# A transformer layer on one core: where the first stage's weight scans and gate sums stand, and which engine makes the bounds of w2 and w_out

## The chip, the core and the metric

The kernel runs on one core of a Trainium2 chip. A core has five engines that run their own queues in order and meet only at semaphores: TensorE (PE: matmul and transpose, into PSUM), VectorE (DVE), ScalarE (ACT), GpSimd (POOL) and SyncE (SP, which here issues most DMAs). An instruction at the head of a queue that waits holds up everything behind it on that engine. The metric is the device time of one execution in microseconds (us); lower is better. All times here are from runs on the chip, and the trace is one profiled execution.

## The reference

One layer (`DEPTH` = 1) with 2048 latent rows and 256 context rows of width 1024. Two mixers read the same projection `h @ w_in`: a retention (linear attention with decay, both directions) and a grouped-query attention; their outputs are joined and go through `w_out`, then a squared-ReLU MLP follows.

```python
mod = (c_act @ w_mod + b_mod)[:, None, :]
sh1, sc1, g1, sh2, sc2, g2 = jnp.split(mod, 6, axis=-1)
h = _modulate(_rmsnorm(x, norm1_g), sh1, sc1)
rq, rk, rv, rg, aq, ak, av = jnp.split(h @ w_in, SPLIT_IDX, axis=-1)
...
x = x + g1 * (jnp.concatenate([ret, att], axis=-1) @ w_out)
h2 = _modulate(_rmsnorm(x, norm2_g), sh2, sc2)
x = x + g2 * _sqrelu_mlp(h2, w_ff1, w_ff2)
```

The context rows need only the columns rk, rv, ak and av.

## The kernel before

The kernel has three stages. The first, some 672 us long, makes `h @ w_in` and everything that later stages need beforehand. The second is the attention with the retention beside it, the third the MLP. The later stages are written out by hand in a fixed order (`manual_schedule`); the first is not. There the program is written as loops, and a list scheduler at build time decides each engine's order: it takes instructions forward as soon as what they need, their buffers among it, is free in its own plan. An operation that depends on nothing but a load and a buffer can so be placed far ahead of the place where it is written.

**Groups and chunks.** The 18 tiles of 128 rows go in three groups: G0 is two context tiles and four latent ones, G1 and G2 are six latent tiles each (`GROUPS`). For each group the columns of w_in are passed in six chunks (`PLAN`): AKV (256 columns: ak and av), AQ, RK, RV, RQ and RG (512 each). G0 begins with RK; G2 ends with RG, RQ. One chunk of one tile, here called a product, is 24 matmuls (`products`, L824 to L826: eight slices of the inner dimension, in three parts of a split into a high and a low half) into one of five PSUM banks `pso`. Then `post` takes it out: an ACT copy `xs` (L524 for RK and RQ, L552 for RV, L556 for RG, L565 for AQ, L586 for AKV), a rotation on DVE and POOL (`rope`, L489 to L496), head norms for AQ and AKV, transposes on PE a tile later (`turn`) and stores by SP.

**What DVE does in this stage.** Beside the rotations: the low halves of the weights (`split_w`, L67, `wlo`), the low halves and the modulation of the next group's `h` (`part_h`, L436 and L67, `lo`), and three kinds of work that no product of this stage needs:

- `weight_maxima`: 72 pieces of weights, 32 of w1, 32 of w2 and 8 of w_out. Each is a DMA of 512 KB into a buffer `wm` (two of them) and a DVE maximum of absolute values into one column of `wmx` (L662). `ff_scales` reads the columns at the start of G2's last chunk and makes powers of two of them, by which the operands of the later stages are scaled.
- `mod_steps`: the later rows of the modulation (gates, second shift and scale). Each is a chain of 16 multiply-adds over a DMA'd piece of w_mod (L354, L356, `macc`), closed by a matmul that sums it over the partitions (L368).
- in G2 alone the attention's values, the decay tables and the first maxima of the attention: `first_maximum` puts 18 pairs of a PE product (L165, L169) and a DVE maximum `nm` (L178) beside G2's last chunks. All 18 share one PSUM bank, so each product waits for the maximum before it.

The loop over chunks and tiles calls one step of `mods` for each tile from G0's second chunk on, apart from G0's last two, and one step of `maxima` for each tile from G1 on (two for the first tile of a chunk):

```python
if mods and (g, c) >= (0, 1) and (g, c) not in ((0, 4), (0, 5)):
    mods.pop(0)()
if (g, c) >= (1, 0):
    for step in maxima[: 1 + (m == 0)]:
        step()
```

The scheduler does not keep the maxima there: a piece depends on its load and on `wm` alone, so in the built program the first stands among G0's first products and the last in G1's RV.

Of the kernel before, what the change touches and what calls it, by code (L numbers as in the profile page):

```python
# [14 lines left out]
BF16 = mybir.dt.bfloat16  # L15
I32 = mybir.dt.int32
AF = mybir.ActivationFunctionType
ALU = mybir.AluOpType
AX = mybir.AxisListType
# [3 lines left out]
P = 128  # L23
D = 1024
# [18 lines left out]
C_RQ, C_RK, C_RV, C_RG, C_AQ, C_AKV = 0, 512, 1024, 1536, 2048, 2560  # L43
# [11 lines left out]
def layer_kernel(ctx: ExitStack, tc: tile.TileContext, a: dict, out: bass.AP):  # L55
    nc = tc.nc
# [56 lines left out]
    wmx = const.tile([P, 88], F32, name="wmx")  # L113
# [27 lines left out]
    class Group:  # L141
# [18 lines left out]
        def piece(self, i, pool=None, tag="mp"):  # L160
            m = self.m[i] = (pool or psS).tile([P, 512], F32, name="mp", tag=tag)
            h, r = i // 9 * 2, i % 9
            if r < 8:
                k = ks[:, self.g, r % 4 * 512 : (r % 4 + 1) * 512]
                mm(m, self.qr[:, 0, h + r // 4], k, start=True, stop=True)  # L165
            else:
                for e in range(2):
                    k = ks[:, self.g, 2048:]
                    mm(m[:, 256 * e : 256 * e + 256], self.qr[:, 0, h + e], k, start=True, stop=True)  # L169
# [90 lines left out]
    with ExitStack() as st:  # L260
# [131 lines left out]
        def mod_steps():  # L392
            steps = later_rows(4, lambda b: store_gate(0, b)) + later_rows(6, shift2)
            return steps + later_rows(8, scale2) + later_rows(10, lambda b: store_gate(1, b))
# [255 lines left out]
        def weight_maxima():  # L650


            def piece(i):
                w = sg.tile([P, D], F32, name="wm", tag="wm", bufs=2)
                if i < 32:
                    src = a["w_ff1"][0, i // 4 * P : (i // 4 + 1) * P, i % 4 * D : (i % 4 + 1) * D]
                elif i < 64:
                    src = a["w_ff2"][0, (i - 32) * P : (i - 31) * P, :]
                else:
                    src = a["w_out"][0, (i - 64) * P : (i - 63) * P, :]  # L660
                nc.sync.dma_start(w, src)
                nc.vector.tensor_reduce(wmx[:, i : i + 1], w, axis=AX.X, op=ALU.max, apply_absolute_value=True)  # L662

            return [lambda i=i: piece(i) for i in range(72)]

        def ff_scales():

# [213 lines left out]
        hs, w, begun = start()  # L881
# [3 lines left out]
        balance(g2)  # L885
        todo = [(g, c) for g in range(len(GROUPS)) for c in range(len(PLAN[g]))]
        spare = []
        mods = mod_steps()
        maxima = weight_maxima()
        beside = None  # L890
        for n, (g, c) in enumerate(todo):
            if (g, c) == (2, 1):
                spare += value_parts()
            if (g, c) == (2, 2):
                spare += decay_tables()
            if (g, c) == (2, 5):
                spare += ff_scales()
            col, width = PLAN[g][c]
            last = c == len(PLAN[g]) - 1
            more = g + 1 < len(GROUPS)  # L900
            w_next = None
            if n + 1 < len(todo):

                w_next = load_w(*PLAN[todo[n + 1][0]][todo[n + 1][1]], range(0, KT if n else 4, 2))
            if more and (c == len(PLAN[g]) - 2):
                loads, xs = load_x(GROUPS[g + 1])
                for load in loads:
                    load()
            nxt = []
            for m, (kind, i) in enumerate(GROUPS[g]):  # L910
                if not (kind == "c" and col in (C_RQ, C_RG, C_AQ)):
                    ps, k = (begun.pop(m), 6) if n == 0 and m in begun else (None, 4)
                    if ps is None:
                        ps = psO.tile([P, 512], F32, name="pso", tag="pso")
                        products(ps, hs[m], w, width, range(4))
                    if beside:
                        next(beside, None)
                    products(ps, hs[m], w, width, range(k, KT))
                    todo_ = later[:]
                    later.clear()  # L920
                    post(col, kind, i, ps)
                    for fn in todo_:
                        fn()
                    if spare:
                        spare.pop(0)()
                    if mods and (g, c) >= (0, 1) and (g, c) not in ((0, 4), (0, 5)):
                        mods.pop(0)()
                    if (g, c) >= (1, 0):
                        for step in maxima[: 1 + (m == 0)]:
                            step()  # L930
                        del maxima[: 1 + (m == 0)]
                    if (g, c, m) == (2, 2, 0):
                        beside = first_maximum()
                if n == 0 and m == len(GROUPS[g]) - 1:
                    w_next += load_w(*PLAN[0][1], range(4, KT, 2))
                if last and more:
                    nxt += make_h(GROUPS[g + 1][m : m + 1], xs[m : m + 1])
            w = w_next
            if last and more:
                hs = nxt  # L940
# [867 lines left out]
```

## Time and profile before

| | |
|---|---|
| median of three runs | 2945.95 us (2940.34 to 2947.11) |
| profiled execution | 2946.76 us |
| its span, first to last instruction | 2945.0 us |
| PE busy | 2776.2 us (94%) |
| DVE busy | 2181.6 us (74%) |
| ACT busy | 1388.0 us (47%) |
| POOL busy | 1550.2 us (53%) |
| DVE maxima of weights (L662) | 72 of 1.211 us, 36 us to 343 us from the start |
| mean granted TensorE clock | 0.987 |

How to read it: an engine's busy time is the sum of its instructions. A PE that is busy all the time need not be at its peak, since a matmul's end is modelled and matmuls overlap; the distance between the starts of two of them is the better measure. Rows of a timeline give start, duration, engine, line, operation, result and operand, count, and in brackets how long the engine sat idle just before and what ended that. Rows of windows give, for each stretch, its length, the busy time (and number) of PE, PE's weight loads, DVE, ACT and POOL, the granted clock, the share of the 16 DMA engines and the GB/s; for a single line they give that engine alone. Rows of waits give total, times and longest.

### The profile page before, as it was taken

What the parts mean: (1) busy time and instruction counts of PE and PEld (TensorE: products, weight loads), DVE (VectorE), ACT (ScalarE), POOL (GpSimd) and SP (SyncE); (2) the same over time, 40 slices, a digit from 0 to 9 for tenths busy, and PEclk for the clock granted to TensorE, in tenths of its full rate; (3) what the DMA queues carried; (4) which work ended last, traced back from release to release, by engine and by line L of the source; (5) the groups of instructions that cost most, each with busy time, mean ns of one, the idle gap of its engine ahead of it and who ended that gap; (6) DMA issues with size and microseconds to landing.
All of it is one profiled execution on the core that took longest, in us unless ns stands there. A gap on an engine that the chain in (4) does not pass through costs nothing. (4 is left out here: it accounts for less than half of the span.)

```text
span 2945.0 us, 45295 instructions
## 1 busy us (share of the span) xinstructions
PE 2776.2 (94%) x17140; PEld 1648.8 (56%) x17140; DVE 2181.6 (74%) x3330; ACT 1388.0 (47%) x2280; POOL 1550.2 (53%) x1274
## 2 busy tenths in 40 slices
PE   7998898998799999999999899999999899999998
PEld 3777677775566666565666444444444344444443
DVE  5889847647987777777876577778777777777776
ACT  2333323325777777787777433333332333333332
POOL 3536326425876667887656656664443444444332
PEclk9999999999999999999999999999999999999999
DMA  9988843426412123332211723331114511111111
GB/s 300 340 283 280 271 154 107 160 67 201 137 46 81 49 63 121 90 104 85 73 63 51 273 92 101 104 102 60 53 51 154 173 60 47 54 51 51 58 44 58
DMA packets 265305, 346.95 MB, mean 118 GB/s; under 512 B 106231, under 2 KB 163831, under 8 KB 263294
## 3 DMA queue, kind: packets, MB, share of 16 engines
q1 hardware_dynamic: 254806, 336.57, 35.2%
q10 hardware_dynamic: 10280, 7.48, 0.9%
q8 instruction: 135, 2.21, 0.3%
q14 instruction: 84, 0.69, 0.1%
HBM read 272.52 MB, written 71.46 MB: 117 GB/s over the span
## 5 line engine op out<-in xcount | busy, mean ns | idle before, releaser
L178 DVE TENSOR_REDUCE nm<-mp 128x1 f32<-128x512 f32 (+1 forms) x576 | 390.9, 685 | 172.6 <-PE mp L165 143.3
L219 POOL TENSOR_TENSOR plo<-p,phi 128x1024 f16<-128x1024 f32 x160 | 353.7, 2212 | 172.9 <-ACT phi L212 139.6
L208 ACT ACTIVATE p<-st 128x512 f32<-128x512 f32 x576 | 338.1, 597 | 188.5 <-PE st L203 118.7
L1582 PE MATMUL pd<-w2hi,uhi 128*128 128x512 f16 x1024 | 388.0, 379 | 12.9 <-DVE acc L1585 12.6
L1583 PE MATMUL pd<-w2lo,uhi 128*128 128x512 f16 x1024 | 388.0, 379 | 0.6 <-DVE w2lo L71 0.6
L1584 PE MATMUL pd<-w2hi,ulo 128*128 128x512 f16 x1024 | 388.1, 379 | 0.0
L1585 DVE SCALAR_TENSOR_TENSOR acc<-pd,sc,acc 128x512 f32<-128x512 f32 x512 | 366.4, 739 | 5.7 <-PE pd L1584 5.6
L1522 PE MATMUL pu<-hf,w1f 128*128 128x512 f16 x896 | 340.1, 380 | 2.5 <-DVE q L1545 2.0
L1523 PE MATMUL pu<-hf,w1f 128*128 128x512 f16 x896 | 340.0, 379 | 0.0
L1524 PE MATMUL pu<-hf,w1f 128*128 128x512 f16 x896 | 339.8, 379 | 0.0
L824 PE MATMUL pso<-whi,hi_l 128*128 128x512 f32 (+1 forms) x768 | 295.8, 388 | 10.2 <-ACT xs L524 4.3
L212 ACT ACTIVATE phi<-p 128x1024 f16<-128x1024 f32 x288 | 303.8, 1055 | 0.0
L826 PE MATMUL pso<-whi,lo_l 128*128 128x512 f32 (+1 forms) x768 | 293.7, 383 | 4.1 <-DVE lo_l L67 4.1
L825 PE MATMUL pso<-wlo,hi_l 128*128 128x512 f32 (+1 forms) x768 | 292.9, 382 | 0.8 <-DVE wlo L67 0.7
L235 PE MATMUL o<-wv,plo 128*128 128x65 f16 x2304 | 235.9, 193 | 23.9 <-POOL plo L219 17.0
L221 DVE TENSOR_TENSOR plo<-p,phi 128x512 f16<-128x512 f32 x256 | 240.9, 942 | 18.6 <-ACT phi L212 15.7
L236 PE MATMUL o<-wv,phi 128*128 128x129 f16 x2304 | 243.8, 221 | 0.0
L235 PEld LDWEIGHTS <-plo 128*128 128x128 f16 x2304 | 206.7, 98 | 59.8 <-POOL plo L219 25.9
L202 PE MATMUL st<-qr,ks 128*128 128x512 f16 x576 | 220.2, 382 | 12.4 <-ACT p L208 10.4
L1534 POOL TENSOR_TENSOR r<-r 128x512 f32<-128x512 f32 x64 | 66.3, 1039 | 295.2 <-ACT r L1533 295.2
L203 PE MATMUL st<-qr,ks 128*128 128x512 f16 x576 | 220.0, 382 | 0.1
L165 PE MATMUL mp<-ks,qr 128*128 128x512 f16 x512 | 196.7, 384 | 23.0 <-DVE nm L178 22.2
(324 smaller groups left out, 5751.4 us busy)
## 6 DMA issues: line engine op xcount, KB each, us to landing
wm<-in_w_ff SPq DMA_DIRECT2D x64, 512.0 KB, 5.3
w1r<-in_w_ff SPq DMA_DIRECT2D x64, 512.0 KB, 4.6
ws<-in_w_ff SPq DMA_DIRECT2D x124, 256.0 KB, 3.5
wst<-in_w_in SPq DMA_DIRECT2D x60, 512.0 KB, 5.5
wst<-in_w_mod SPq DMA_DIRECT2D x32, 512.0 KB, 6.0
hf<-hp SPq DMA_DIRECT2D x56, 256.0 KB, 3.2
hf<-hf SPq DMA_DIRECT2D x14, 1024.0 KB, 7.1
orv<-rv SPq DMA_DIRECT2D x35, 256.0 KB, 4.0
```

Source lines behind the costliest of these rows:

```text
L178: nc.vector.tensor_reduce(dst, src, axis=AX.X, op=ALU.max, negate=True)
L208: nc.scalar.activation(self.p[kt // 2][:, kt % 2], self.s.pop(kt), AF.Exp, scale=HD**-0.5)
L212: nc.scalar.activation(hi, self.p[j], AF.Copy)
L219: nc.gpsimd.tensor_tensor(lo, p, hi, op=ALU.subtract)
L235: mm(o[:, : HD + 1], lo[:, i, c], v[:, : HD + 1], start=False, stop=False)
L1522: mm(pu[i], whi, hi, start=k == 0, stop=False)
L1523: mm(pu[i], whi, lo, start=False, stop=False)
L1524: mm(pu[i], wlo, hi, start=False, stop=k == 3)
L1582: mm(ps, uh, wh, start=f == 0, stop=False)
L1583: mm(ps, uh, wl, start=False, stop=False)
L1584: mm(ps, ul, wh, start=False, stop=f == NF - 1)
L1585: nc.vector.scalar_tensor_tensor(acc[:, c], ps, sc2, acc[:, c], op0=ALU.mult, op1=ALU.add)
```

## The change

Three things, all in the first stage.

- The 40 pieces of w2 and w_out are no longer scanned for a maximum on DVE. ACT takes the absolute value of each piece with its accumulator on (L668), so that the column holds the sum of magnitudes of a row, which bounds the maximum from above. The elementwise result goes into `junk`, a buffer of one that the squares of `load_x` and the head norms use too. The load into `wm` stays.
- The 32 maxima of w1 (L665) and all of `mod_steps` become one list, `extra`, with the mod steps first. Each slot (a tile of a chunk from G0's second chunk to G2's RG) earns credit in proportion to a number given for its chunk (`ROOM`; less where the next group's `h` is made beside it), and steps are taken from the list while the credit lasts. AKV earns nothing.
- The bounds on ACT are called one for each tile from G1 on, except in AKV.

Since `wm` has two buffers and `junk` one, and both are now shared by instructions of two engines in the order of the program, the scheduler can't take the w1 maxima ahead of the bounds that come before them.

```diff
                 nc.sync.dma_start(w, src)
-                nc.vector.tensor_reduce(wmx[:, i : i + 1], w, axis=AX.X, op=ALU.max, apply_absolute_value=True)
-
-            return [lambda i=i: piece(i) for i in range(72)]
+                to = wmx[:, i : i + 1]
+                if i < 32:
+                    nc.vector.tensor_reduce(to, w, axis=AX.X, op=ALU.max, apply_absolute_value=True)
+                else:
+                    junk = tp.tile([P, D], BF16, name="junk", tag="junk", bufs=1)
+                    nc.scalar.activation(junk, w, AF.Abs, accum_out=to)
+
+            steps = [lambda i=i: piece(i) for i in range(72)]
+            return steps[:32], steps[32:]
...
-        mods = mod_steps()
-        maxima = weight_maxima()
+        ROOM = {C_AKV: 0.0, C_AQ: 0.2, C_RK: 1.2, C_RV: 4.2, C_RQ: 3.4, C_RG: 3.2}
+        maxima, bounds = weight_maxima()
+        extra = [(1.56, fn) for fn in mod_steps()] + [(1.2, fn) for fn in maxima]
+
+        def room(g, c):
+            v = ROOM[PLAN[g][c][0]]
+            return v - 2.2 if c == len(PLAN[g]) - 1 and g + 1 < len(GROUPS) else v
...
+        slots = [(g, c) for g, c in todo if (0, 1) <= (g, c) < (2, 5)]
+        share = sum(x for x, _ in extra) / sum(room(*s) * len(tiles_of(*s)) for s in slots)
+        credit = 0.0
...
-                    if mods and (g, c) >= (0, 1) and (g, c) not in ((0, 4), (0, 5)):
-                        mods.pop(0)()
-                    if (g, c) >= (1, 0):
-                        for step in maxima[: 1 + (m == 0)]:
-                            step()
-                        del maxima[: 1 + (m == 0)]
+                    if (g, c) in slots:
+                        credit += share * room(g, c)
+                        while extra and credit > -0.01:
+                            cost, fn = extra.pop(0)
+                            credit -= cost
+                            fn()
+                        if g > 0 and col != C_AKV and bounds:
+                            bounds.pop(0)()
```

In the built program the change shows at three places. The first is DVE's queue where G0's RG meets G1's first chunk. `t` and `lo` belong to the next group's `h`, `wlo` to the next chunk's weights, `wmx<-ys` to RG's own rows. Before:

```order
L436 TENSOR_TENSOR t<-psx,a_237 128x512 x2
L662 TENSOR_REDUCE wmx<-wm 128x1 x2
L67 TENSOR_TENSOR lo_l_2108<-t,hi_l_2107 128x512
L67 TENSOR_TENSOR lo_l_2130<-t,hi_l_2129 128x512
L662 TENSOR_REDUCE wmx<-wm 128x1
L436 TENSOR_TENSOR t<-psx,a_237 128x512
L662 TENSOR_REDUCE wmx<-wm 128x1
L67 TENSOR_TENSOR wlo<-wst,whi 128x2x256
L559 TENSOR_REDUCE wmx<-ys 128x1
```

Now the same place, with the multiply-adds of the modulation between:

```order
L436 TENSOR_TENSOR t<-psx,a_237 128x512
L356 SCALAR_TENSOR_TENSOR macc<-wst,cc,macc 128x512
L67 TENSOR_TENSOR lo_l_2117<-t,hi_l_2116 128x512
L356 SCALAR_TENSOR_TENSOR macc<-wst,cc,macc 128x512
L67 TENSOR_TENSOR lo_l_2139<-t,hi_l_2138 128x512
L436 TENSOR_TENSOR t<-psx,a_237 128x512
L67 TENSOR_TENSOR lo_l_2139<-t,hi_l_2138 128x512
L436 TENSOR_TENSOR t<-psx,a_237 128x512
L559 TENSOR_REDUCE wmx<-ys 128x1
```

The maxima of weights are gone from between the steps of `h`: from G0's RG to the end of G1's AKV before has 16 of them, the program now none, with about as many multiply-adds (8 and 6).

The second place is ACT's queue in G1's RK. `xs` takes a product out of PSUM, `zs` a transposed tile; `qh` is AQ's. Before:

```order
L577 ACTIVATE qh<-psx 128x512
L66 ACTIVATE whi<-wst 128x1024 x2
L546 ACTIVATE zs<-psx 128x512
L515 DMA rtb<-in_ret_cs 128x256
L524 ACTIVATE xs<-pso 128x512
L546 ACTIVATE zs<-psx 128x512
```

Now:

```order
L668 ACTIVATE junk,wmx<-wm 128x1024
L577 ACTIVATE qh<-psx 128x512
L524 ACTIVATE xs<-pso 128x512
L668 ACTIVATE junk,wmx<-wm 128x1024
L546 ACTIVATE zs<-psx 128x512
L515 DMA rtb<-in_ret_cs 128x256
L668 ACTIVATE junk,wmx<-wm 128x1024 x2
```

From G1's AQ to its RV the queue now holds 26 such bounds, one or two ahead of each copy.

The third place is DVE's queue in G2's RV, where the first maxima of the attention (`nm`) run. Before:

```order
L496 TENSOR_TENSOR ys<-t_5644,t_5645 128x512
L178 TENSOR_REDUCE nm<-mp 128x1 x5
L67 TENSOR_TENSOR wlo<-wst,whi 128x1024
L178 TENSOR_REDUCE nm<-mp 128x2
L67 TENSOR_TENSOR wlo<-wst,whi 128x1024 x3
```

Now:

```order
L178 TENSOR_REDUCE nm<-mp 128x1
L496 TENSOR_TENSOR ys<-t_5639,t_5640 128x512
L665 TENSOR_REDUCE wmx<-wm 128x1
L178 TENSOR_REDUCE nm<-mp 128x1
L665 TENSOR_REDUCE wmx<-wm 128x1
L178 TENSOR_REDUCE nm<-mp 128x1
L665 TENSOR_REDUCE wmx<-wm 128x1 x2
L178 TENSOR_REDUCE nm<-mp 128x1
L665 TENSOR_REDUCE wmx<-wm 128x1 x3
```

Of the 32 maxima of w1, 29 now stand after the first product of G2's RK, 24 of them in RV and RG, each waiting for a load of its own; three stand in G1's RQ. Of the 64 multiply-adds, 16 stand in G1's RQ and RG, where before had 4.

More of the change, by code (lines that the diff above doesn't have):

```diff
@@ L887, in layer_kernel, with tiles_of @@
         spare = []
-        mods = mod_steps()
-        maxima = weight_maxima()
+        ROOM = {C_AKV: 0.0, C_AQ: 0.2, C_RK: 1.2, C_RV: 4.2, C_RQ: 3.4, C_RG: 3.2}
[4 more added lines that the diff above has]
+            return v - 2.2 if c == len(PLAN[g]) - 1 and g + 1 < len(GROUPS) else v
+        def tiles_of(g, c):
+            return [t for t in GROUPS[g] if not (t[0] == "c" and PLAN[g][c][0] in (C_RQ, C_RG, C_AQ))]
+        slots = [(g, c) for g, c in todo if (0, 1) <= (g, c) < (2, 5)]
+        share = sum(x for x, _ in extra) / sum(room(*s) * len(tiles_of(*s)) for s in slots)
+        credit = 0.0
         beside = None
@@ L896, in layer_kernel @@
             if (g, c) == (2, 5):
+                assert not extra and not bounds, (len(extra), len(bounds))
                 spare += ff_scales()
```

## The prediction

> **What bounds the kernel now.** I read the page's slices first, to see where PE is not full, then tables by stretches of the first stage, and then the waits and the timeline inside the worst stretch.
>
> ```profile
> PE 2776.2 (94%) x17140; PEld 1648.8 (56%) x17140; DVE 2181.6 (74%) x3330; ACT 1388.0 (47%) x2280; POOL 1550.2 (53%) x1274
> ...
> PE   7998898998799999999999899999999899999998
> ...
> DVE  5889847647987777777876577778777777777776
> ```
>
> A slice is 73.6 us. PE is the bound nearly everywhere; its weak slices are the first nine, and there, in slices 2 to 4, DVE is at eight and nine tenths. To cut the first stage into chunks I use ACT's copies out of `pso`: the first copy of a chunk marks where its first product has ended.
>
> ```profile
> 204.85 0.59 ACT L556 ACTIVATE xs<-pso 128x512 f32<-128x512 f32 x1
> ...
> 277.83 0.60 ACT L565 ACTIVATE xs<-pso 128x512 f32<-128x512 f32 x1 [4.24 <-PE pso L826]
> ...
> 398.50 0.60 ACT L524 ACTIVATE xs<-pso 128x512 f32<-128x512 f32 x1 [5.36 <-DMA rv<-xs]
> ...
> 431.85 0.60 ACT L556 ACTIVATE xs<-pso 128x512 f32<-128x512 f32 x1 [3.29 <-PE pso L826]
> ...
> 490.36 0.60 ACT L565 ACTIVATE xs<-pso 128x512 f32<-128x512 f32 x1 [2.85 <-PE pso L826]
> ...
> 536.67 0.60 ACT L524 ACTIVATE xs<-pso 128x512 f32<-128x512 f32 x1 [0.83 <-PE pso L826]
> 573.50 0.60 ACT L552 ACTIVATE xs<-pso 128x512 f32<-128x512 f32 x1 [3.02 <-PE pso L826]
> ...
> 591.09 0.60 ACT L552 ACTIVATE xs<-pso 128x512 f32<-128x512 f32 x1 [5.12 <-PE pso L826]
> 596.80 0.60 ACT L552 ACTIVATE xs<-pso 128x512 f32<-128x512 f32 x1 [5.12 <-PE pso L826]
> 609.51 0.60 ACT L556 ACTIVATE xs<-pso 128x512 f32<-128x512 f32 x1
> 642.52 0.60 ACT L524 ACTIVATE xs<-pso 128x512 f32<-128x512 f32 x1 [5.11 <-PE pso L826]
> ```
>
> The rows at 591.09 and 596.80 are two products that wait for PE alone: one product of 512 columns takes 5.71 us, one of 256 half of that, 2.86. That is the yardstick. Now the busy times, first of all work (PE, weight loads, DVE, ACT, POOL), then of the weight maxima alone (DVE):
>
> ```profile
> 0.00:85.00 85.00, 66.65 (x328) 38.57 (x329) 47.36 (x100) 26.24 (x50) 23.79 (x43) 0.98 0.93 315
> 85.00:204.85 119.85, 113.87 (x584) 93.48 (x583) 108.08 (x144) 46.07 (x81) 59.21 (x64) 1.00 0.91 306
> 204.85:277.83 72.98, 63.27 (x331) 52.31 (x330) 67.42 (x97) 21.82 (x44) 38.93 (x46) 0.91 0.90 297
> 277.83:398.50 120.67, 110.41 (x480) 86.50 (x479) 86.50 (x111) 39.76 (x61) 44.36 (x44) 0.94 0.75 244
> 398.50:469.40 70.90, 68.84 (x355) 56.93 (x354) 39.98 (x52) 23.81 (x38) 34.53 (x29) 1.00 0.40 121
> 469.40:536.67 67.27, 59.32 (x314) 50.63 (x313) 51.46 (x123) 31.55 (x68) 43.60 (x55) 0.95 0.31 90
> 536.67:672.00 135.33, 133.91 (x613) 106.72 (x612) 63.71 (x126) 34.00 (x49) 35.13 (x36) 1.00 0.38 123
> ```
>
> ```profile
> 0.00:85.00 85.00, 12.10 (x10) 0.98 0.93 315
> 85.00:204.85 119.85, 33.18 (x28) 1.00 0.91 306
> 204.85:277.83 72.98, 22.46 (x19) 0.91 0.90 297
> 277.83:398.50 120.67, 19.35 (x16) 0.94 0.75 244
> ```
>
> From 85 to 278 us DVE is busy 90 to 92% of the time, and a third of that is weight maxima; from 398 us on there are none and DVE has room. One maximum is 1.21 us, one multiply-add of the modulation 0.78:
>
> ```profile
> L662 DVE TENSOR_REDUCE wmx<-wm 128x1 f32<-128x1024 f32 x72 | 87.1, 1211 | 14.8 <-DMA wm<-in_w_ff 11.4 <-DMA wm<-in_w_out 3.3
> ...
> L356 DVE SCALAR_TENSOR_TENSOR macc<-wst,cc,macc 128x512 f32<-128x512 f32 x56 | 43.7, 781 | 7.9 <-DMA wst<-in_w_mod 7.2
> ```
>
> In the worst stretch, G0's RG and G1's AKV (204.85 to 277.83), PE's waits all lead back to DVE's queue:
>
> ```profile
> PE pso L826 <- DVE lo_l L67: 4.1, 3, 2.0
> PE pso L824 <- ACT hi_l L66: 2.6, 2, 2.2
> PE psx L434 <- DVE t L436: 2.0, 2, 1.7
> ```
>
> `lo` and `t` are the next group's `h`, and the ACT operation between them waits for `t` by way of POOL. The waits are 8.7 us, yet the stretch loses more, because TensorE runs at half pace after them:
>
> ```profile
> 238.29 0.58 PE L826 MATMUL pso<-whi,lo_l 128*128 128x256 f32 x1 [2.00 <-DVE lo_l L67]
> 238.67 0.41 PE L824 MATMUL pso<-whi,hi_l 128*128 128x256 f32 x1
> 238.88 0.41 PE L825 MATMUL pso<-wlo,hi_l 128*128 128x256 f32 x1
> ...
> 242.09 0.28 PE L824 MATMUL pso<-whi,hi_l 128*128 128x256 f32 x1
> 242.22 0.28 PE L825 MATMUL pso<-wlo,hi_l 128*128 128x256 f32 x1
> ```
>
> Starts are 0.21 us apart after the wait of 2.00 us, 0.12 to 0.13 us apart three and a half us later; the stretch's granted clock is 0.91.
>
> **The change part by part.** The sum is made against the profiled execution's 2946.76 us, which is 0.8 us over the median of the runs, 2945.95.
>
> *Term 1, G0's RG and G1's AKV.* The same pair of chunks in the next group, RG and AKV from 431.85 to 490.36, has no weight maxima and takes 58.5 us with two products of 512 columns more, so 58.5 - 2 x 5.71 = 47.1 us is what 73.0 us would come down to. DVE's part falls from 67.4 by the 22.5 us of maxima to 45, with about as many multiply-adds as before. 45 of 47 us is tight, so I leave 4 us of waits: 73 - 51 gives -22. Bounds: -26 (no wait left) and -9 (only the waits named go, the clock stays).
>
> One rule of the Trainium skill speaks against the larger value: TensorE: Matmul & The Clock Gate, Part 1, says that the clock falls to half after an idle window of about 3.4 us, and no wait here is longer than 2.2. By it the half pace would have another cause and would stay, and the term would be 0.09 x 73 = 6.6 us smaller, -15. The trace shows the half pace right behind waits of 2 us, so I do not follow it.
>
> *Term 2, G1's AQ, RK and RV* (277.83 to 398.50, 120.7 us). G2's RK and RV, 536.67 to 609.51, take 36.4 us each without maxima; three such are 109.2. DVE loses 16 maxima (19.4 us) and a dozen multiply-adds. ACT gains 26 bounds. The nearest operation in the trace is the square with accumulator over the same 1024 columns, with its read:
>
> ```profile
> L410 ACT ACTIVATE junk<-x_l x16: 1039/1057/1061, 23.4 to 320.3; 128x1024 bf16<-128x1024 f32 x16
> L410 ACT ACTIVATION_READ_ACCUMULATOR junk<-x_l x16: 185/186/203, 24.4 to 321.3; 128x1 f32 x16
> ```
>
> 26 x 1.24 = 32 us raises ACT from 40 to 72 of 110 us, so the time itself is covered by PE. What is behind each bound on ACT is a copy out of `pso` or `psx`; five `pso` banks are 28 us of cover for the first, two `psx` banks little for the second. So -10, with bounds -15 and +16 (below).
>
> *Term 3, the first 205 us.* 85.00 to 204.85 holds some six small and fifteen large products, 6 x 2.86 + 15 x 5.71 = 103 us of 120, some 5 us of it finishing RK. DVE falls from 108 to 75 us, 90% to 62%. Of about 12 us I take 8 (two thirds, as DVE is not the only thing late there). In the first 85 us ten maxima and their 5.2 MB of DMA leave, at 315 GB/s 17 us of DMA time; but PE's clock there is 0.98, and the loads that go ahead were queued behind those that PE needs. I take 0, bounds 0 and -6. Term 3 is -8, from -18 to 0.
>
> *Term 4, G1's RQ and RG.* DVE gains 12 multiply-adds of 0.78 us and three maxima, 13 us on 40 of 71; PE covers it. ACT gains four bounds, 5 us on 24. G2's AKV and AQ lose nothing, since no maxima were there, and gain five bounds on ACT, 6 us on 32 of 67. 0 for both.
>
> *Term 5, G2's RK, RV, RG and RQ.* 29 maxima of 1.21 us put 35 us on DVE's 64 of 135, which PE's pace covers, provided that their loads come in time: RV and RG hold 24, from 573.50 to 642.52, 2.9 us each. Two buffers give one piece per half of (landing + 1.21).
>
> ```profile
> DMA to landing us min/median/max: 3.3/5.3/9.1
> ...
> DMA to landing us min/median/max: 4.1/5.1/5.3
> ```
>
> The first row is `wm` as it was loaded before, between full DMA engines; the second is w_in's pieces of the same size from 529 to 640 us, the nearer one. By 3.3, 4.1, 5.1 and 9.1 us a piece takes 2.3, 2.7, 3.2 and 5.2 us; 24 pieces are late by 0, 0, 7 and 55 us. Lateness counts because the attention's first maxima (`nm`) and the next `wlo` stand behind a waiting piece on DVE, and PE's next L165 waits for `nm`. The median row is of loads issued in threes and fours at once; these go one by one, so I lean to 4.1 and take +4, bounds 0 and +55. SP's queue holds the same loads between the stores of rv and rg, where each can hold them back for a us or two: inside the +4. POOL's queue holds none of it.
>
> The Trainium skill, DMA: Bandwidth & Descriptors, Anatomy of one DMA, fits a DMA on GpSimd's path as 2.0 us and the bytes at 436 GB/s. An estimate by that page is 3.2 us for 512 KB, and by it term 5 would be 0. The shortest row, 3.3 us, agrees; the medians do not.
>
> *Term 6, the later stages.* Their order is written by hand and unchanged; the scales are read from the same columns at the start of RQ. 0.
>
> Sum: -22 - 10 - 8 + 0 + 4 = -36, so 2946.76 - 36 = 2910.8, and by the median's 0.8 less 2910.0.
>
> **The rivals.**
> *ACT takes the wait over.* If the bounds wait for loads as long as 7 us, RK's twelve take 12 x (7 + 1.24) / 2 = 49 us in a chunk of 36, and the transposes' copies wait behind them. Then term 2 turns to 0, and term 3 and 5 halve and double: -22 - 4 + 8 = -18, 2928. For it: ACT and DVE now share two buffers in one order, and `wm` did land as late as 9.1 us. Against it: that was between full DMA engines, and from 277.83 to 398.50 the DMA share was 0.75 with 16 pieces of `wm` in it; there will be 26, but they are called one a tile, not as fast as buffers come free.
> *A larger gain.* All of the room between the stretches and their yardsticks is taken, -26 - 15 - 18 = -59, and loads come in time: 2887. For it speaks DMA's 0.93 at the start; against it that DVE stays tight in term 1.
> *The loads of w1 pace G2 and the kernel is slower.* With 9.1 us of landing RV and RG last 55 us longer: -40 + 55 = +15, 2961. It decides from (69 + 40) / 24 x 2 - 1.21 = 7.9 us of landing on. For it: DVE waits in order and a single PSUM bank ties PE to it. Against it: the DMA share is 0.38 there, where nothing landed later than 5.3 us.
> *Nothing.* The waits go by POOL instead, which stands between `t` and `hi`, and DVE's relief is hidden: 2946. Against it: POOL is busy 38.9 of 73 us.
>
> **How the numbers follow.** The forecast (2900 to 2922) 0.53, ACT's waits 0.18, the larger gain 0.11, nothing 0.05, slower 0.13. Under 0.3%, 9 us, a measurement of this kernel can hardly tell from no change. Faster is 0.53 + 0.18 + 0.11 = 0.82, same 0.05, slower 0.13. The range leaves out the slower case, nothing, and the end of the larger gain: 2891 to 2936.
>
> **What would show it.** Right: from G0's RG to G1's AQ some 50 us instead of 73 and a clock near 1.00 there; DVE at 60 to 65% from 85 us to RG; G1's chunks as long as G2's; PE's end of the first stage near 636 us. Wrong: ACT's bounds waiting for `wm` with PE's transposes behind; DVE's L665 waiting for DMA in G2's RV and RG by more than a few us, and L165 behind L178.

## The result and the profile after

| | before | after |
|---|---|---|
| median of ten runs each | 2946.48 us (2940.34 to 2949.63) | 2952.84 us (2948.55 to 2961.59) |
| span of the profiled execution | 2945.0 us | 2950.2 us |
| ratio after / before | | 1.0031, 95% interval 1.0021 to 1.0041 |

The changed kernel is slower by 0.31%, where 1.2% faster was forecast. The page of the changed kernel, engines and slices:

```profile
PE 2769.6 (94%) x17140; PEld 1643.3 (56%) x17140; DVE 2151.8 (73%) x3290; ACT 1430.9 (49%) x2360; POOL 1555.0 (53%) x1274
...
PE   7999998988789998999999899999999999999998
...
DVE  4668468667987777777877477778777777777776
```

DVE's load did move: its slices 2 to 4 (eight, eight and nine tenths before) are at six, six and eight. PE's eights in the fourth and fifth slice are gone, but the ninth, 590 to 664 us, has become one. The first copies of the chunks out of `pso`, cut as in the prediction (ACT's timeline of the changed kernel):

```profile
202.13 0.60 ACT L556 ACTIVATE xs<-pso 128x512 f32<-128x512 f32 x1 [1.70 <-DMA qt<-zs]
...
256.24 0.58 ACT L565 ACTIVATE xs<-pso 128x512 f32<-128x512 f32 x1
...
375.87 0.58 ACT L524 ACTIVATE xs<-pso 128x512 f32<-128x512 f32 x1
...
447.41 0.39 ACT L586 ACTIVATE xs<-pso 128x256 f32<-128x256 f32 x1 [0.51 <-PE pso L833]
...
523.40 0.59 ACT L524 ACTIVATE xs<-pso 128x512 f32<-128x512 f32 x1
...
646.79 0.60 ACT L524 ACTIVATE xs<-pso 128x512 f32<-128x512 f32 x1 [6.11 <-PE pso L833]
...
676.85 0.60 ACT L524 ACTIVATE xs<-pso 128x512 f32<-128x512 f32 x1 [3.08 <-PE pso L833]
```

The last row is the last copy of the stage; before it stood at 672.1 us. By stretches between these rows (us):

| stretch | before | after | moved | forecast |
|---|---|---|---|---|
| to G0's RG (term 3) | 204.8 | 202.1 | -2.7 | -8 |
| G0's RG, G1's AKV (term 1) | 73.0 | 54.1 | -18.9 | -22 |
| G1's AQ, RK, RV (term 2) | 120.7 | 119.6 | -1.0 | -10 |
| G1's RQ, RG (term 4) | 70.9 | 71.5 | +0.6 | 0 |
| G2's AKV, AQ (term 4) | 67.3 | 76.0 | +8.7 | 0 |
| G2's RK, RV, RG and RQ to the last copy (term 5) | 135.4 | 153.4 | +18.0 | +4 |
| from the last copy to the end of the span (term 6) | 2272.9 | 2273.4 | +0.5 | 0 |

The sum is +5.2 us, the difference of the spans (the medians differ by 6.4). Busy times of the changed kernel in the same stretches (PE, weight loads, DVE, ACT, POOL, then clock, DMA share, GB/s):

```profile
85.00:202.13 117.13, 113.51 (x579) 93.41 (x578) 80.60 (x120) 45.48 (x79) 53.43 (x61) 0.99 0.62 195
202.13:256.24 54.11, 48.74 (x296) 42.64 (x295) 42.65 (x67) 20.84 (x41) 38.85 (x45) 0.97 0.62 192
256.24:375.87 119.63, 111.82 (x502) 86.56 (x501) 68.22 (x88) 67.56 (x116) 47.86 (x45) 1.00 0.79 263
375.87:447.41 71.54, 69.47 (x347) 56.43 (x347) 50.83 (x62) 25.40 (x42) 31.95 (x27) 1.00 0.66 219
447.41:523.40 75.99, 66.82 (x349) 56.18 (x349) 61.65 (x133) 38.73 (x79) 48.69 (x60) 0.96 0.50 132
523.40:646.79 123.39, 107.73 (x450) 84.31 (x449) 72.62 (x85) 31.15 (x47) 23.68 (x20) 0.93 0.74 241
```

The seam between G0 and G1 did what term 1 says: 54.1 us, clock 0.97. The last row is the new worst stretch: PE is busy 107.7 of 123.4 us, DVE only 72.6, and the clock is 0.93. DVE is not full there, it waits. The waits of that stretch, and the landings of `wm` in it:

```profile
DVE wmx L665 <- DMA wm<-in_w_ff: 40.7, 24, 3.6
ACT junk L668 <- DMA wm<-in_w_out: 11.1, 3, 4.5
PE mp L165 <- DVE nm L178: 9.6, 5, 3.7
```

```profile
DMA to landing us min/median/max: 4.5/5.3/7.4
```

24 maxima wait for their loads, 40.7 us in all, and five times PE waits for a maximum of the attention (`nm`) that stands right behind one of them. DVE's timeline in G2's RG shows the order:

```profile
612.09 1.22 DVE L665 TENSOR_REDUCE wmx<-wm 128x1 f32<-128x1024 f32 x1 [2.33 <-DMA wm<-in_w_ff]
615.48 1.22 DVE L665 TENSOR_REDUCE wmx<-wm 128x1 f32<-128x1024 f32 x1 [2.17 <-DMA wm<-in_w_ff]
616.62 0.68 DVE L178 TENSOR_REDUCE nm<-mp 128x1 f32<-128x512 f32 x1
```

And PE's timeline behind that `nm`:

```profile
617.36 0.38 PE L165 MATMUL mp<-ks,qr 128*128 128x512 f16 x1 [2.52 <-DVE nm L178]
...
620.20 0.63 PE L831 MATMUL pso<-whi,hi_l 128*128 128x512 f32 x1
620.62 0.63 PE L832 MATMUL pso<-wlo,hi_l 128*128 128x512 f32 x1
...
621.68 0.40 PE L832 MATMUL pso<-wlo,hi_l 128*128 128x512 f32 x1
621.92 0.40 PE L833 MATMUL pso<-whi,lo_l 128*128 128x512 f32 x1
```

A wait of 2.5 us is followed by some 3.5 us in which matmuls start 0.42 us apart instead of 0.23: the half pace that the prediction showed at the seam before now stands in G2.

### The profile page after: what moved, and what is told of

Read it like the earlier page. It is cut to its first block, busy times and chain, and to the rows that moved or that the text cites. A ratio compares the mean times of both kernels' runs of the same rounds, so it can differ in the third digit from the quotient of the medians.

```text
span 2950.2 us, 45373 instructions
## 1 busy us (share of the span) xinstructions
PE 2769.6 (94%) x17140; PEld 1643.3 (56%) x17140; DVE 2151.8 (73%) x3290; ACT 1430.9 (49%) x2360; POOL 1555.0 (53%) x1274
## 5 line engine op out<-in xcount | busy, mean ns | idle before, releaser
L235 PEld LDWEIGHTS <-plo 128*128 128x128 f16 x2304 | 205.6, 98 | 58.6 <-POOL plo L219 26.0
L202 PE MATMUL st<-qr,ks 128*128 128x512 f16 x576 | 219.0, 380 | 16.5 <-ACT p L208 16.3
L1558 POOL TENSOR_TENSOR r<-r 128x512 f32<-128x512 f32 x64 | 66.4, 1041 | 294.5 <-ACT r L1557 294.5
```

The lines of the kernel that those rows point to most:

```text
L235: mm(o[:, : HD + 1], lo[:, i, c], v[:, : HD + 1], start=False, stop=False)
```

## The experiments

Verdicts of single runs go by the end of the first stage (its last copy), because the rest of the program, which is the same everywhere, took from 2272.6 to 2282.1 us in the profiled executions. Four kernels built nearly alike up to G2's RK reach it at 523.4, 526.2, 527.7 and 528.6 us, so a difference below some 5 us at that place says little. In every run the stretches are cut at the same copies (us):

| kernel | time | to G0's RG | G0 RG, G1 AKV | G1 AQ to RV | G1 RQ, RG | G2 AKV, AQ | G2 RK to RG | last copy |
|---|---|---|---|---|---|---|---|---|
| before | 2946.5 | 204.8 | 73.0 | 120.7 | 70.9 | 67.3 | 105.8 | 672.1 |
| after | 2952.8 | 202.1 | 54.1 | 119.6 | 71.5 | 76.0 | 123.4 | 676.9 |
| w1_eight_columns | 2953.8 | 204.5 | 56.5 | 118.8 | 71.0 | 77.0 | 112.6 | 669.9 |
| w1_eight_loads | 2938.9 | 202.9 | 56.3 | 118.9 | 74.9 | 73.1 | 103.2 | 659.5 |
| halves | 2942.3 | 200.1 | 55.8 | 117.1 | 72.3 | 79.0 | 113.4 | 667.6 |
| w1_noop | 2936.4 | 205.1 | 55.2 | 120.4 | 73.6 | 74.2 | 102.2 | 660.4 |
| no_w1 | 2923.2 | 197.4 | 52.1 | 116.4 | 70.6 | 72.6 | 108.1 | 646.6 |
| no_scans_after | 2924.5 | 199.2 | 51.5 | 107.1 | 76.2 | 71.6 | 106.1 | 641.2 |
| before_no_scans | 2918.9 | 194.3 | 54.0 | 113.2 | 72.9 | 69.6 | 109.2 | 643.0 |
| before_act | 2935.4 | 203.1 | 55.5 | 114.1 | 71.5 | 74.4 | 106.2 | 654.4 |
| before_act_in_place | 2929.9 | 210.0 | 69.9 | 100.3 | 72.2 | 65.6 | 107.2 | 654.8 |
| in_place | 2937.3 | 220.2 | 64.0 | 100.3 | 77.2 | 67.9 | 106.4 | 665.6 |
| gate | 2948.9 | 194.0 | 58.1 | 137.4 | 66.4 | 80.6 | 103.8 | 669.9 |
| w1_in_g1 | 2937.3 | 194.9 | 58.6 | 137.8 | 57.4 | 72.9 | 108.1 | 659.7 |
| before_act_halves | 2936.4 | 206.7 | 66.2 | 108.6 | 71.3 | 68.0 | 106.0 | 656.4 |

The theories, as the expectations name them: LOADS (w1's loads, through two buffers, set the pace of G2), ACT (the sums on ScalarE wait for loads and for the shared scratch `junk`, with the copies behind them), WORK (VectorE's own time for the scans).

### What costs in G2: four edits of the changed kernel

*w1_eight_columns*: loads kept, the scans nearly taken away; 1016 of 1024 columns are left out of w1's bound.

```diff
-nc.vector.tensor_reduce(to, w, axis=AX.X, op=ALU.max, apply_absolute_value=True)
+nc.vector.tensor_reduce(to, w[:, :8], axis=AX.X, op=ALU.max, apply_absolute_value=True)
```

> The changed kernel, with each maximum of w1 taken over the first 8 of its 1024 columns (the other 1016 are left out of the bound); every load of 512 KB stays and DVE waits for it as before. Theory LOADS (G2 is late because DVE stands waiting for w1's pieces, which two buffers deliver one in 3.2 us, with nm and wlo behind it): G2's RG stays near 47 us, and the kernel near 2950, 2944 to 2953. Theory WORK (the 35 us of DVE work of these maxima make G2 late): RG falls to some 35 us and the kernel to 2925 to 2932.

*w1_eight_loads*: the scans kept, three loads of four taken away; 24 pieces of w1 are left out of its bound.

```diff
+kept = []
 def piece(i):
+    if i < 32 and i % 4:
+        nc.vector.tensor_reduce(
+            wmx[:, i : i + 1], kept[0], axis=AX.X, op=ALU.max, apply_absolute_value=True
+        )
+        return
     w = sg.tile([P, D], F32, name="wm", tag="wm", bufs=2)
+    kept[:] = [w]
...
```

> The changed kernel with all its 32 maxima of w1 on VectorE, but a load for every fourth alone: each loaded piece is scanned four times (24 of 32 pieces of w1 are left out). 28 of these maxima now stand in G2's RK and RV, one to RG. LOADS (the pace of w1's loads through two buffers, with the attention's `nm` and `wlo` behind on VectorE): the stage ends like the version without w1's scans, last copy at 647 to 653 us (the changed kernel 676.9; without w1 646.6), RG2 33 to 35 us. WORK (39 us of VectorE's own time in G2): last copy still at 665 us or later.

*halves*: the same bytes in twice as many loads.

```diff
-w = sg.tile([P, D], F32, name="wm", tag="wm", bufs=2)
+w = sg.tile([P, 512], F32, name="wm", tag="wm", bufs=4)
...
-steps = [lambda i=i: piece(i) for i in range(72)]
+steps = [lambda i=2 * i: (piece(i), piece(i + 1)) for i in range(72)]
...
```

> The changed kernel with every piece of 512 KB loaded and scanned as two halves of 256 KB, in four buffers of half the size (the same bytes, the same room in SBUF, the same places in the order; nothing is left out). LOADS by latency (a landing is mostly a fixed time, so four smaller loads in flight bring more bytes): a half lands in 3.3 to 4 us, a pair of halves comes every 2.0 to 2.4 us instead of 3.2, RG2 36 to 39 us and the last copy at 660 to 668 us. LOADS by rate (the bytes take the time, whatever their number): a half lands in some 5 us, RG2 stays at 44 to 48 us and the last copy at 675 us or later, since 64 scans of half the length cost VectorE a little more.

*w1_noop*: w1's scans and loads gone, so that its bound is left out, and all else in its place.

```diff
-return steps[:32], steps[32:]
+nc.vector.memset(wmx[:, :32], 1.0)
+return [lambda: None] * 32, steps[32:]
```

> The changed kernel with w1's 32 maxima and loads taken out and nothing else moved: their places stay counted, so the modulation's multiply-adds stay where the changed kernel has them (32 of them in G0, where the version without w1 had 20 there). w1's bound is left out. The changed kernel reaches G2's RK at 523.4 us, the version without w1 at 509.1. If the denser multiply-adds cost these 14 us: RK at 518 to 524 us, RK to RG about 104 to 108 us, last copy at 655 to 660 us. If it was w1's three early scans and its loads in G1's RQ and G2's AQ: RK at 508 to 513 us, last copy at 645 to 650 us.

Busy times from the first copy of G2's RK to the first of its RQ, in w1_noop:

```profile
528.60:630.80 102.20, 99.54 (x450) 78.88 (x449) 39.73 (x55) 30.11 (x46) 20.67 (x19) 1.00 0.43 140
```

and w1_eight_loads:

```profile
526.20:629.50 103.30, 99.22 (x442) 79.17 (x441) 65.65 (x78) 29.05 (x44) 18.95 (x19) 0.98 0.53 172
```

DVE works 39.7 us in the one and 65.7 us in the other, and the stretch is as long: VectorE's time for w1 costs nothing by itself in G2, though in w1_eight_loads it stands in RK and RV only. With the loads it is 123.4 us. Taking the scans nearly away and leaving the loads regains only half of that (112.6):

```profile
527.70:640.30 112.60, 101.95 (x448) 79.78 (x447) 40.58 (x82) 29.95 (x45) 19.89 (x19) 0.98 0.77 257
```

So WORK falls and LOADS stands for this part: 676.9 - 660.4 = 16.5 us of stage end. How the other half of the 21 us arises is argued: a piece still takes a buffer for its landing and DVE still stands waiting, but the DMA engines also carry more than in w1_noop (share 0.77 against 0.43), and no run has the one without the other. The waits of w1_eight_columns in the stretch and of halves; first the one, then the other:

```profile
DVE wmx L665 <- DMA wm<-in_w_ff: 55.9, 25, 3.7
...
PE mp L165 <- DVE nm L178: 5.2, 3, 2.8
```

```profile
DVE wmx L665 <- DMA wm<-in_w_ff: 24.3, 24, 3.0
...
PE mp L165 <- DVE nm L178: 5.4, 3, 2.1
```

Of halves the landings from 560 to 638 us:

```profile
DMA to landing us min/median/max: 2.9/3.8/7.2
```

Half the bytes land in 3.8 us where the whole took 5.3, so a pair of halves comes faster: 48 of them start from 560.5 to 623.2 us, 2.7 us a pair, where the changed kernel's 24 from 562.8 to 636.6 us are 3.2 us apart. That is LOADS by latency, as the last copy at 667.6 us is, with less to gain than expected (2.0 to 2.4 us a pair, RG2, which is G2's RG, 36 to 39 us; it was 40.2). The other three miss their values too. w1_eight_columns has the time that LOADS gave, but its RG2, 40.5 us, lies between the 47 of LOADS and the 35 of WORK. w1_eight_loads ends its stage at 659.5 us, between 653 and 665. w1_noop is up to 5 us later at RK than expected for denser multiply-adds, and its RK to RG is 2 us shorter.

w1_noop also says where the rest lies. It still reaches G2's RK at 528.6 us and ends 13.8 us behind no_w1 (below), and the two differ in nothing but where the multiply-adds of the modulation stand: 32 of them have run ahead of G1's AQ here, 21 there.

### What the sums on ScalarE and the multiply-adds cost

*no_w1*: the changed kernel without w1's pieces (its bound is left out), whose places are given to the multiply-adds.

```diff
-return steps[:32], steps[32:]
+nc.vector.memset(wmx[:, :32], 1.0)
+return [], steps[32:]
```

> The changed kernel without its 32 maxima of w1 and without the loads that they read (their columns are filled with 1.0, so w1's bound is left out); the 40 bounds on ScalarE stay, with their loads. LOADS (the two-buffer pace of w1's loads costs G2's RK, RV and RG): G2's RV and RG return to 36 and 33 us (from 37.2 and 45.8). ACT (the bounds wait for loads and for `junk` on ScalarE): G1's AQ to RV stay near 119 us and G2's AKV and AQ near 76 us (the kernel before: 67), since nothing is taken from ScalarE there. Then the time is 2953 - 14 = 2939. If ScalarE's bounds were not to blame, AKV and AQ would return to 67 as well, and the time would be 2930.

*no_scans_after*: the sums taken away too, so that all four bounds are left out.

```diff
-return steps[:32], steps[32:]
+nc.vector.memset(wmx[:, :72], 1.0)
+return [], []
```

> The changed kernel with no scan of a weight at all (all 72 columns are 1.0; the bounds of all four matrices are left out), so that of the change only the new places of the modulation's multiply-adds are left. Beside the kernel before without scans (2918.9). If the new places of the multiply-adds cost nothing by themselves, it is 2919 within 4 us, and all of the loss of the changed kernel comes from where the scans stand. If they cost, it is 2925 or more, in G1's RG and G2's chunks.

*before_no_scans*: the kernel before without any scan, all four bounds left out.

```diff
-return [lambda i=i: piece(i) for i in range(72)]
+nc.vector.memset(wmx[:, :72], 1.0)
+return []
```

> The kernel before without any of the 72 scans and their loads (the columns are filled with a constant, so the scales are not those of the weights). What the scans cost in all: by my sum of the stretches against their yardsticks 40 us, 2903 to 2910. If the waits are those of POOL or of the loads of w_in instead, 2930 to 2945.

before_no_scans was expected at 2903 to 2910 us and took 2918.9: all 72 scans together cost 29.1 us of stage end (672.1 - 643.0), not 40. no_w1 came 16 us below the one reading of its expectation and 7 below the other. ScalarE's sums do wait in it, in G1's AQ to RV, as they do in the changed kernel; the waits of no_w1, then of the changed kernel in that stretch:

```profile
ACT junk L668 <- DMA wm<-in_w_ff: 27.1, 14, 2.8
...
ACT junk L668 <- DVE hs_q L503: 10.0, 6, 3.4
```

```profile
ACT junk L668 <- DMA wm<-in_w_ff: 27.0, 13, 3.9
...
ACT junk L668 <- DVE hs_q L503: 13.0, 6, 3.4
```

The same 37 to 40 us of waiting, and yet no_w1 ends its first stage only 5.4 us behind no_scans_after (646.6 against 641.2). The stretch itself is 9 us longer with the sums (116.4 against 107.1) and the next one 6 us shorter. So ACT as a main cause falls. The multiply-adds cost nothing when no scan is there to push them together: no_scans_after ends at 641.2 us and before_no_scans at 643.0; that its time is 5.6 us longer lies wholly behind the first stage (2281.4 against 2274.0 us), where both run the same order.

What pushes them together is the changed kernel's credit, which counts w1's 32 maxima behind the 64 multiply-adds: the more is on the list, the faster its head is taken. In w1_noop's first chunks some of the multiply-adds wait longer for their loads, and so do the weights that are loaded through the same tag `wst`; waits from 85 to 200 us of w1_noop, then of no_w1:

```profile
DVE macc L356 <- DMA wst<-in_w_mod: 13.8, 4, 5.1
...
ACT whi L66 <- DMA wst<-in_w_in: 8.3, 4, 4.7
```

```profile
DVE macc L356 <- DMA wst<-in_w_mod: 5.5, 3, 3.1
...
ACT whi L66 <- DMA wst<-in_w_in: 2.8, 2, 2.3
```

Most of the loss stands at one place, from the first copy of G0's RQ to that of G1's AKV; w1_noop, then no_w1:

```profile
174.63:233.05 58.42, 52.44 (x275) 42.10 (x274) 40.93 (x49) 17.90 (x28) 24.78 (x20) 1.00 0.67 212
```

```profile
173.60:221.05 47.45, 47.45 (x249) 39.43 (x248) 32.11 (x41) 18.09 (x28) 22.42 (x20) 1.00 0.58 188
```

14 multiply-adds run there in the one and six in the other, and this repeats: 55.5 to 58.4 us in the five kernels with 14 (after, w1_noop, w1_eight_columns, w1_eight_loads, halves), 47.3 us in no_scans_after with six and in before_no_scans with none. So what costs is that they stand here, and not their number ahead of G1's AQ, which is 32 in before_no_scans too. That their loads are the way in which it costs is argued from these rows and was not tried by itself. Over the stretches of the table the loss is +7.7, +3.1, +4.0, +3.0 and +1.6 us, and 5.9 us of it are regained from G2's RK to RG, where no_w1 still has multiply-adds.

Together, the last copy of the changed kernel is 35.7 us behind that of no_scans_after: 5.4 for the sums, 13.8 for the places of the multiply-adds, 16.5 for w1's pieces. The kernel before pays 29.1 for its scans.

*before_act*: the kernel before, with nothing but the change of engine for the 40 sums.

```diff
-nc.vector.tensor_reduce(wmx[:, i : i + 1], w, axis=AX.X, op=ALU.max, apply_absolute_value=True)
+to = wmx[:, i : i + 1]
+if i < 32:
+    nc.vector.tensor_reduce(to, w, axis=AX.X, op=ALU.max, apply_absolute_value=True)
+else:
+    junk = tp.tile([P, D], BF16, name="junk", tag="junk", bufs=1)
+    nc.scalar.activation(junk, w, AF.Abs, accum_out=to)
```

> The kernel before with its 40 sums of magnitudes on ScalarE, written to the shared scratch `junk` as the changed kernel does; no other edit. Beside the same kernel with the sums written in place (2929.9). ACT, by way of `junk`: the single scratch holds the bounds back until G1's RK and G2, with w1's loads behind them, and G2's AKV, AQ and RK are longer than 67 and 37 us by some 5 to 10 us in all: 2935 to 2945. If `junk` does not matter, 2930 within 4 us.

*before_act_in_place*: the same with the magnitudes written back into `wm`.

```diff
-    junk = tp.tile([P, D], BF16, name="junk", tag="junk", bufs=1)
-    nc.scalar.activation(junk, w, AF.Abs, accum_out=to)
+    nc.scalar.activation(w, w, AF.Abs, accum_out=to)
```

> The kernel before with one part of the change alone: the 40 bounds of w2 and w_out on ACT, in place; calls and modulation as before. DVE loses 48 us of maxima from G0's RG on, the first 195 us are as before. By both theories the stretch from G0's RG to G1's AKV falls from 73 to some 54 us and nothing else changes: 2925 to 2932. If ACT's waits for its loads hold back the copies behind them (theory ACT), 2936 to 2946.

Both end the stage 17 us earlier than the kernel before, 654.4 and 654.8 us, and so half a microsecond from each other: in sum `junk` does not matter (what G1's AQ to RV and G2's AKV and AQ lose by it, 14 and 9 us, G0 and the seam gain, 7 and 14), though the times, 2935.4 and 2929.9, differ as the expectation had it for the case that it does; the difference lies behind the first stage. Where the scans stand is very different in the two, as the tile `wm` shows, in before_act and in before_act_in_place:

```profile
L667 ACT ACTIVATE junk<-wm x40: 1042/1057/1061, 301.5 to 573.6; 128x1024 bf16<-128x1024 f32 x40
...
L664 DVE TENSOR_REDUCE wmx<-wm x32: 1201/1208/1220, 38.0 to 182.4; 128x1 f32<-128x1024 f32 x32
```

```profile
L666 ACT ACTIVATE wm<-wm x40: 1040/1058/1065, 188.2 to 334.4; 128x1024 f32<-128x1024 f32 x40
...
L664 DVE TENSOR_REDUCE wmx<-wm x32: 1202/1209/1221, 36.1 to 182.6; 128x1 f32<-128x1024 f32 x32
```

In both, w1's maxima are over by 184 us. before_act_in_place has the time expected (2925 to 2932), but by luck: the seam was to fall from 73 to 54 us and is 69.9, and the gain stands in G1's AQ to RV, 100.3 us for 120.7. It is the fastest kernel here that leaves nothing out: 2929.86 us, ratio to before 0.9943, 95% interval 0.9928 to 0.9958.

### Other places for the same scans

*in_place*: the changed kernel with the magnitudes written into `wm`, the edit just shown. Without the hold of `junk` the build takes the sums forward to 35 to 217 us and w1's maxima to 144 to 325 us.

> The changed kernel, with ACT writing the absolute values back into wm and not into junk. In the built program this alone moves the maxima of w1 from G2 to G0 and G1 (8 in G0, 24 from G1's AKV to RK) and the bounds to the first 230 us on ACT, since nothing but loads and wm holds them any more. Theory LOADS: G2 loses its 25 us, G0 and G1 keep most of their 21 us as DVE has only 9 maxima instead of 16 in G0's RG and G1's AKV; 2925 to 2932. Theory ANYWHERE (the maxima cost the same wherever they stand, so what G2 gains G1 loses): 2942 to 2952.

2937.33 us, ratio 0.9965 (0.9953 to 0.9976). G2's RK to RG is back at 106.4 us, and the first 220 us pay 18 us of it. The time lies between the two that were expected (2925 to 2932, 2942 to 2952) and decides for neither.

*gate*: the kernel before with the 40 sums on ScalarE in place, the two `wm` held till G1's AKV, then two pieces a tile, DVE's and ScalarE's alternating.

```diff
+def gate(ps):
+    for _ in range(2):
+        w = sg.tile([P, D], F32, name="wm", tag="wm", bufs=2)
+        nc.scalar.activation(w[:, :256], ps[:, :256], AF.Copy)
...
-if (g, c) >= (1, 0):
-    for step in maxima[: 1 + (m == 0)]:
+if (g, c, m) == (1, 0, 4):
+    maxima.pop(0)(ps)
+if (g, c, m) >= (1, 0, 4):
+    for step in maxima[:2]:
...
```

> The kernel before with the 40 sums on ScalarE in place, maxima of w1 and w2 and the sums alternating, and the two buffers `wm` held until the fourth tile of G1's first chunk, so that no scan is taken during the first 250 us (then two a tile, all of them ahead of G2's RK). It keeps what each kernel had right: G0 and its seam as without scans (205 to 196 us, 73 to 55), G2's RK on as before (36, 36, 33). LOADS and ACT both say that scans cost least when DVE and ScalarE share the pace and w1's loads are over before G2's RK: G1's AQ to RV 115 to 120, G2's AKV and AQ 70, 2920 to 2928, below the 2929.9 of the version in place. WORK (what counts is the busy time of DVE alone, wherever it lies): no better than 2930.

*w1_in_g1*: the same gate, then w1's maxima one a tile in G1's AQ to RQ, and the sums, through `junk`, in G2.

```diff
+if (g, c) >= (1, 1):
+    n_ = 1 + (m == 0 if g == 1 else m % 3 == 0)
+    for step in maxima[:n_]:
...
```

> The kernel before with the 40 sums on ScalarE (through `junk`), none of the scans before G1's AQ (the two buffers `wm` are held by a copy of G1's AKV till then): w1's 32 maxima at one a tile in G1's AQ to RQ, where the load pace is no limit (3.7 us apart), and the sums one a tile in G2's AKV to RV. Nothing is left out. LOADS (w1 costs where it comes faster than its loads, and in-order VectorE makes PE wait): the seam as without scans (52 to 56 us), AQ to RV 115 to 122 us, G2's RK to RG 108 to 112, last copy at 650 to 656 us, 2925 to 2931 and so about the same as the version in place, 2929.9. If w1 costs 30 us wherever its 32 loads stand, the last copy is at 668 us or later and the time 2940 or more.

Both miss, and in the same stretch: G1's AQ to RV takes 137 us in both, with 18 of w1's maxima and 19 sums in gate and 29 maxima in w1_in_g1. gate is 2948.86 us, ratio 1.001 (1.000 to 1.002); w1_in_g1 2937.34 us, ratio 0.9965 (0.9951 to 0.9978), since its next stretch is 14 us shorter than before's. The busy times of that stretch, gate, then w1_in_g1:

```profile
252.00:390.00 138.00, 126.64 (x550) 97.15 (x549) 96.16 (x120) 58.67 (x100) 45.65 (x44) 0.98 0.90 300
```

```profile
253.50:391.40 137.90, 123.45 (x528) 96.53 (x527) 105.63 (x131) 43.10 (x69) 45.98 (x44) 0.94 0.84 287
```

DVE is busy 96 and 106 of 138 us (86.5 of 120.7 in the kernel before), and DMA moves 300 and 287 GB/s, as in that kernel's crowded stretches. The pace of a piece in 3.7 us, which was to be slow enough for the loads, did not make w1 cheap. gate came out as WORK had it (no better than 2930), so WORK falls only for G2; w1_in_g1 ends its stage at 659.7 us, short of the 668 that a fixed price of w1 asked for. Which of DVE's and DMA's queues delays PE in this stretch was not told apart.

*before_act_halves*: before_act_in_place with the halves of the experiment above.

> The kernel before with the 40 sums on ScalarE in place (2929.9) and every piece loaded and scanned as two halves of 256 KB in four buffers of half the size; nothing is left out. If the pace of loads still holds it back where w1's and w2's pieces stand in G0 (0 to G0's RG 210 us, without scans 194): 2920 to 2927. If what it loses there is VectorE's and the DMA queues' time and not the wait for single loads: 2928 to 2934, as in place.

2936.44 us, ratio 0.9965 (0.9955 to 0.9975), last copy 656.4 us: no gain, and above both values expected. That speaks against the wait for single loads as what the scans still cost in G0; but halving also doubles the number of loads, and what that costs was not measured.

## Why the prediction was wrong

The forecast asked for more than there was. Leaving out all 72 scans ends the stage 29.1 us earlier; -36 was forecast with all of them kept. In before_no_scans the stretches of terms 1 to 3 do fall by 37.0 us together, near the -40 forecast, but the later ones grow by 7.9 even without any scan.

*Term 5* failed most, by 14 us; with its +4 the measured rest would have been 9 us faster than before. It said that 24 pieces in G2's RV and RG come 2.9 us apart, that the landing would lean to 4.1 us, and took +4. The landing was 5.3 us in the median, which is the prediction's own other row (5.1); by its law a piece then comes every (5.3 + 1.22) / 2 = 3.26 us, and 3.2 was measured. Those 0.3 us on 24 pieces are the 7 us that the prediction had worked out and set aside. By chunks the loss is 3.6 us in RK (clock 0.92), 1.1 in RV (1.00) and 12.8 in RG (0.89). The rest of the 18 us it did not have at all: term 1 counted the half pace of TensorE behind waits of two microseconds as a loss that goes, and term 5 did not count the same loss as coming back. The clock of 0.93 over 123.4 us is 8.6 us; 7 and 8.6 make most of the 18. The runs show the cause: 102.2 us without w1's scans and loads, clock 1.00, 103.2 with the scans and a quarter of the loads, 123.4 with all. This split of it is worked out, not tried. That VectorE's 35 us of scans are covered by PE was right.

*Term 1* was right in place, mechanism and about in size: -18.9 for -22, and PE's waits on `lo` are gone from the seam. Some 4 us of the seam's RG are the multiply-adds that stand there (27.8 us to G1's AKV, 23.6 in no_w1). The Trainium skill (TensorE: Matmul & The Clock Gate, Part 1) has the clock fall to half after an idle window of about 3.4 us; by that rule the prediction had -15. The trace is nearer to the row than to the rule, since the seam's clock rose to 0.97 when its waits went; the half pace behind the wait of 2.52 us in G2 speaks for the row too.

*Term 2* failed: -1 for -10. DVE was relieved by 18 us (86.5 to 68.2), where the term's maxima and multiply-adds come to 29. The sums on ScalarE wait there, and take 9 us in that stretch, of which the next gives 6 back.

*Term 3* was too large, -2.7 for -8: DVE's 108 us became 80.6 and not 75, since 28 multiply-adds stand ahead of G0's RG and not 24 (21.5 us for 17.4). Term 3 does not have these four at all. The ten in G0's RQ stand where that chunk takes 27.8 us, 23.8 in no_w1 with six.

*Term 4* failed in G2's AKV and AQ, +8.7 for 0. There is one w1 scan in it, at its end, and without any scan it is still 71.6 us in the new order, 69.6 in the old one, so about half of it belongs to the scans and their loads at most; the rest stays open. *Term 6*, 0, was right.

The terms before G2's RK gave -40 and came to -13; of these 27 us, w1_noop against no_w1 shows up to 19.5 us (528.6 and 509.1 at G2's RK) that hang on the places of the multiply-adds alone; 8 to 11 of them repeat in five kernels.

Of the rivals, the loads of w1 pacing G2 is what happened, though its price was not: it asked for landings of 7.9 us, since it set the full gain of 40 us against them. Against the 13 us that came its law asks for 5.6 us; with 5.3 the kernel would still have been 4 us faster, and the half pace, which the law does not have, made up the difference. That ScalarE takes the wait over is true of the wait and not of the price (27 us of waiting, 5 us of stage). The estimate by the Trainium skill (DMA: Bandwidth & Descriptors, Anatomy of one DMA), 3.2 us for 512 KB, was below every landing of `wm` from G2's RK to RG (4.5 to 7.4 us); the measurement decides, and by it term 5 could not be 0. One reading of the slices was incomplete: PE is also weak in the tenth and eleventh before (eight and seven tenths, 663 to 810 us), behind the first stage, where the change does nothing.

## What to carry to other kernels

Work that is covered by an engine's room is covered only as fast as its loads come: divide landing plus scan by the number of buffers, compare it with the pace at which the pieces are called, and take the landing's median in a stretch like the new one, not the lower one that suits. Measure first what leaving the work out altogether gains (29 us here), and do not forecast more than that for moving it. If a short wait makes TensorE run slower for microseconds after it, count that wherever a wait is put as well as where one is taken away. And an item added to a list that is paced by its length also moves all that stands ahead of it: here that went with some 14 us, about as much as the item itself.

## What was not expected of the hardware

A load of half the size is not twice as fast: 256 KB landed in 3.8 us in the median and 512 KB in 5.3, so four small buffers bring the same bytes every 2.7 us where two large ones bring them every 3.2. Why is not shown. The part of the program behind the first stage, the same in order in all these kernels, took 2273 to 2282 us from one profiled execution to the next, more than the changed kernel lost.
